# Hybrid decoder layer: gated results over the recurrence's and the convolution's tiles, squares in a buffer of their own

## The chip, the cores and the metric

One core of one Trainium2 chip runs the whole layer as one program. The metric is the device time of one execution in microseconds (us). The core has a matrix engine (TensorE, PE in the profile; its weight loads are PEld), a vector engine (VectorE, DVE), an engine for functions of one operand (ScalarE, ACT), a general engine (GpSimd, POOL), and SyncE (SP), which here issues nearly all transfers (DMA) between the chip's large memory (DRAM) and the on-chip tiles. Each engine executes its own instructions strictly in the order of the program; engines wait for each other by semaphores.

## What is computed

```python
D_MODEL, BATCH, SEQ = 1024, 1, 2048     # D_CONV = D_LRU = 1024
xn = rms_norm(x, ln_g)
proj = einsum('bsd,de->bse', xn, w_in)                  # 1024 -> 6144 columns
b_gate, c_gate, x_conv, g_conv, x_lru, g_lru = split(proj)
y_conv = b_gate * causal_depthwise_conv(c_gate * x_conv, conv_w)             # width 3
y_conv = headwise_rms_norm(y_conv, 8, conv_out_g) * silu(g_conv)
u = causal_depthwise_conv(x_lru, lru_conv_w) + lru_conv_b                    # width 4
r, i = sigmoid(heads(u) @ w_a + b_a), sigmoid(heads(u) @ w_i + b_i)
a = exp(8 * r * log_sigmoid(lam))
h_t = a_t * h_(t-1) + sqrt(1 - a_t^2) * (i_t * u_t)                          # scan over positions
y_lru = headwise_rms_norm(h, 16, lru_out_g) * silu(g_lru)
out = rms_norm(x + concat(y_conv, y_lru) @ w_out, final_g)
```

All of it is float32. The change concerns the two `headwise_rms_norm(...) * silu(...)`: the mean of squares of a head, and the product of a mixer's result with its gain and its gate. The factor 1/rms of a head is applied later, when the products are read back for the output projection.

## The kernel before

**Tiles and steps.** The channels lie on the 128 partitions, positions along a tile. The positions go in two halves of 1024, `h` = 0 and 1. A half of one block of 128 channels is a 128x1024 float32 tile. Float32 products are built from three matmuls of split operands (a high part `th` or `s`, a low part `tl`), and blocks of matrices are combined so that seven products do the work of eight (a step). There are 64 steps: in each half and for each of the eight channel blocks `k` a triple of three steps, `l` (columns of the recurrence and its gate), `a` and `b` (the convolution's columns and its gate); after the two halves 16 steps `o` of the output projection. A step has seven slots, one for each product (the eighth pass of a step's loop, where there is one, falls together with the next step's first); a triple has 21 slots. The first half splits its weights on the way, the second half reads the split inputs back from DRAM (`s<-sd`).

**What sets the order.** It is written by hand. `tick()` (L151) is called at each slot and issues what was put off by `at(n, f)`, n slots ago. The results of a product are combined by ACT copies (`q`, `u`, `rr`, L1234 to L1240) and DVE additions (`gl`, `gb`, `xl`, ... `<-bank`, L163) and so free the PSUM banks that TensorE writes next. Everything that is late on these two engines therefore reaches TensorE by way of `bank`.

**The tiles around the change.** In a triple, `lru` (L638) makes the recurrence: gates on TensorE (L680), Tanh, Exp and Sqrt on ACT, then on DVE the scan into tile `r` (one buffer, L714). `conv_a` and `conv_b` make the convolution's result in tile `t` (one buffer). The gates go to tiles `gl` (recurrence) and `gb` (convolution), which share two buffers and take turns; `silu` (L608) makes `g * sigmoid(g)` of them, with ACT for the sigmoid `sg` (L613, behind a table load) and POOL for the product.

`finish` (L593) ends a mixer's block: for the recurrence it is called at slot 17 after its last input and so acts from slot 2 of the next triple (`d0` = 0); for the convolution it is called with `d0` = 6 and acts from slot 7 of the next triple. It issues, in order of slots: `f1` (L595, DVE), the product of result, gain and gate, written over the gate tile; `store` (L600, SP), which writes that product to `yd` in DRAM in two transfers; the Square (L605, ACT), written over the result `y`; and `head_sums` (L586, DVE), a sum over channels of a head with a transposing reduction, whose input is read with a stride of 32 elements (128 bytes). When all 16 sums of a half are there, `head_norms` makes 1/rms with a few matmuls (`norm_ps`) and stores it to `rsd`.

**The ring "hl".** Four buffers of 128x1024 are handed out in turn under the tag `hl`: for the inputs at the start (`xrow`, `xcol`), the two `st` tiles of each recurrence, and the `so` tiles of `jobs`. `jobs()` (L363) prepares, during the second half from step 30 on, inputs of the output projection: it reads `yd` and `rsd` back, multiplies, combines, and for seven tiles in each of six jobs casts to a `so` tile (L421, ACT), subtracts (DVE) and stores it two slots later (L426, SP). `hl_tile` counts the tiles in use and `may()` (L352) holds a job's next tile back while the count is at 4 (at 2 in places 20 and 0 to 2 of a triple, and always in places 8 to 12):

```python
    def hl_tile(name, n=1):
        hlc[0] += n
        return [wt("hl", name, dt=F32R, bufs=HL) for _ in range(n)]

    def may():
        p = place[0]
        if 8 <= p <= 12:
            return False
        return hlc[0] < (2 if p >= 20 or p <= 2 else 4)
```

At the turn from the first half to the second, and from the second to the output projection, ACT also casts the next stage's weights (`th<-traw`, L280 and L458) and DVE makes their low parts (`tl`).

Of the kernel before, what the change touches and what calls it, by code (L numbers as in the profile page):

```python
# [12 lines left out]
F32 = mybir.dt.float32  # L13
F32R = mybir.dt.float32r
AF = mybir.ActivationFunctionType
# [5 lines left out]
C = 512  # L21
NC = S // C
NB = C // P
KT = D // P
EPS = 1e-6
PE = mybir.EngineType.PE
R = 32
# [11 lines left out]
def hymba_kernel(ctx: ExitStack, tc: tile.TileContext, x, xt, w_in, par, lamc, w_gate, w_out, final_g, out):  # L39
    nc = tc.nc  # L40
# [21 lines left out]
    def wt(tag, name, n=2 * C, dt=F32, bufs=1):  # L62
        return work.tile([P, n], dt, tag=tag, bufs=bufs, name=name)

    IG, O2, HL = 2, 2, 4
# [30 lines left out]
    for w in range(2):  # L96
        nc.gpsimd.tensor_tensor(out=sel[0][:, w * R:(w + 1) * R], in0=quarter[2 * w],
                                in1=quarter[2 * w + 1], op=ALU.add)
    nc.gpsimd.tensor_tensor(out=sel[1][:, 2 * R:], in0=sel[0].bitcast(F32)[:, 0:R],
                            in1=sel[0].bitcast(F32)[:, R:2 * R], op=ALU.add)  # L100
# [8 lines left out]
    hl = const.tile([P, KT], F32, name="hl")  # L109
# [34 lines left out]
    def at(slots, *fs):  # L144
        if slots == 0:
            for f in fs:
                f()
        else:
            due.append([slots, fs])
# [188 lines left out]

    hlc = [0]

    def hl_tile(name, n=1):
        hlc[0] += n
        return [wt("hl", name, dt=F32R, bufs=HL) for _ in range(n)]

    def hl_done(n):
        hlc[0] -= n
# [16 lines left out]
    def jobs():  # L363
        tjobs = [(t, j) for t in (2, 3) for j in range(NB)]
        for ph, m in ((0, 0), (0, 1), (1, 0), (1, 1), (0, 2), (0, 3)):
# [42 lines left out]
            for n, (i, v, after) in enumerate(items):  # L408
                if prev:
                    prev()  # L410
                    prev = None
                if n in (1, 5):
                    sums()
                if n in (2, 6):
                    more()
                if n == 4:
                    blocks()
                while not may():
                    yield
                t, = hl_tile("so")  # L420
                nc.scalar.copy(t[:, 0:C], v)  # L421

                def prev(t=t, i=i, v=v, after=after, dst=so[ph, m]):
                    tt(t[:, C:2 * C], v, t[:, 0:C].bitcast(F32), ALU.subtract)
                    after()
                    at(2, lambda: nc.sync.dma_start(  # L426
                        dst[i], t.bitcast(F32).rearrange("p (h c) -> p h c", h=2)))
                    at(3, lambda: hl_done(1))

                yield  # L430
# [111 lines left out]
    sums, summed = [None], [0]  # L542

    def head_norms(h):
        sm_ = sums[0]
        rt, = hl_tile("rt")
        rh, rl = rt[:, 0:C], rt[:, C:2 * C]
        at(4, lambda: hl_done(1))
        v = {}

        def split():
            nc.scalar.copy(rh, sm_)
            tt(rl, sm_, rh.bitcast(F32), ALU.subtract)

        def add():
            v["ps"] = pss.tile([P, C], F32, tag="s", name="norm_ps")[:NR, 0:KT * R]
            parts = [(n, q) for n in range(2) for q in (rh, rl)]
            for m, (n, q) in enumerate(parts):
                nc.tensor.matmul(v["ps"], sel[n], q[:, (1 - n) * KT * R:(2 - n) * KT * R],
                                 start=m == 0, stop=m == 3)  # L560

        def root():
            v["rs"] = aux("hn")[:NR, 0:KT * R]
            nc.scalar.activation(out=v["rs"], in_=v["ps"], func=AF.Sqrt, scale=inv_hd, bias=eps[:NR])

        def store():
            for w in range(3):
                k0 = (w + 1) % 3 * KT
                for i in range(2):
                    for b in range(NB):  # L570
                        p0 = w * R + (i * NB + b) * 4
                        nc.sync.dma_start(
                            rsd[h][i, b, k0:k0 + KT, :].rearrange("k (q r) -> q k r", q=4),
                            v["rs"][p0:p0 + 4].rearrange("q (k r) -> q k r", k=KT))
            normed[h] = True

        split()
        at(2, add)
        at(3, root)
        at(4, lambda: nc.vector.reciprocal(out=v["rs"], in_=v["rs"]))  # L580
        at(5, store)

    def head_sums(h, kt, y):
        if summed[0] == 0:
            sums[0] = psn.tile([P, 2 * KT * R], F32, tag="sums", name="sums")
        nc.vector.tensor_reduce(out=sums[0][:, kt * R:(kt + 1) * R], in_=y.rearrange("p (a r) -> p r a", r=R),  # L586
                                axis=mybir.AxisListType.X, op=ALU.add, apply_transpose=True)
        summed[0] += 1
        if summed[0] == 2 * KT:
            summed[0] = 0  # L590
            at(1, lambda: head_norms(h))

    def finish(d0, h, kt, y, sil, gain):  # L593
        def f1():
            nc.vector.scalar_tensor_tensor(out=sil, in0=y, scalar=gain, in1=sil,  # L595
                                           op0=ALU.mult, op1=ALU.mult)

        def store():
            for i in range(2):
                nc.sync.dma_start(yd[2 * h + i][:, :, kt, :].rearrange("b p t -> p b t"),  # L600
                                  sil[:, i * C:(i + 1) * C].rearrange("p (b t) -> p b t", b=NB))

        at(d0, f1)
        at(d0 + (1 if kt == KT and h == 0 else 2), store)
        at(d0 + 2, lambda: nc.scalar.activation(out=y, in_=y, func=AF.Square))  # L605
        at(d0 + 3, lambda: head_sums(h, kt, y))

    def silu(g, late=0):  # L608
        sg = [None]
# [28 lines left out]
    def lru(h, k, late=0):  # L638
# [22 lines left out]
        def sth():  # L661
            v["st"] = st = hl_tile("st", 2)
            at(6, lambda: hl_done(2))
            for j, hi in enumerate((LO, HI)):
                nc.scalar.copy(st[j][hi], v["u"][hi])
# [53 lines left out]
        def out_():  # L719
            finish(0, h, KT + k, v["r"], g, pt[:, LG + k:LG + k + 1])  # L720
# [65 lines left out]
    def conv_b(h, k):  # L786
        g = wt("o2", "gb", bufs=O2)

        def put(which, bank, other):
            t = tcur["t"]  # L790
            if which == 11 and other is None:
                tt(t[:, 0:C], bank, t[:, 0:C], ALU.mult)
            elif which == 11:
                tt(other, bank, other, ALU.add)
                tt(t[:, 0:C], other, t[:, 0:C], ALU.mult)
            elif which == 12 and other is None:
                tt(t[:, C:N2], bank, t[:, C:N2], ALU.mult)
            elif which == 12:
                tt(other, bank, other, ALU.add)
                tt(t[:, C:N2], other, t[:, C:N2], ALU.mult)  # L800
            else:
                combine(g[:, 0:C] if which == 21 else g[:, C:N2], bank, other)
            if which == 21:
                silu(g)
                finish(6, h, k, t, g, pt[:, CG + k:CG + k + 1])

        return put
# [126 lines left out]
    with tc.manual_schedule(engines={ENG.PE, ENG.Activation, ENG.DVE, ENG.Pool, ENG.SP}):  # L934
# [176 lines left out]
        for n in range(PLAIN, N):  # L1111
            kind, h, k = steps[n]
# [52 lines left out]
            for s in range(8 if new or last else 7):  # L1165
                i = ((0, 6) + ORDER[1:])[s]
# [59 lines left out]
                b = {0: "A", 1: "A", 2: "A", 5: "A", 3: "B", 6: "B", 4: "C"}[i]  # L1226
# [71 lines left out]
```

## Time and profile before

| | us |
|---|---|
| time before, median of 3 runs | 1403.29 (1401.82 to 1404.75) |
| the profiled execution | 1404.29 |
| its span in the trace | 1402.2 |

| engine | busy, us | share of the span |
|---|---|---|
| TensorE matmul | 1309.4 | 93% |
| VectorE | 1071.1 | 76% |
| ScalarE | 749.3 | 53% |
| GpSimd | 225.9 | 16% |

The granted TensorE clock was 0.981 of full speed on average. In the rows that follow, a group has line, engine, operation, tiles and shapes, then count, busy time, mean ns of one and the idle time ahead of it with its releasers. A row of the timeline has start, duration, engine, line, operation, tiles, and in brackets the idle time ahead of it and what ended it.

### The profile page before, as it was taken

The numbers are of one execution on the slowest core, as the hardware profiler recorded it, in microseconds if no ns is written. First come the engines' busy times: TensorE is split into PE (matmuls) and PEld (weight loads), VectorE is DVE, ScalarE is ACT, GpSimd is POOL, SyncE is SP. The second block draws the span as 40 slices with busy tenths as digits, with TensorE's granted clock in tenths as the row PEclk, the third lists the DMA queues.
The fourth block names the chain that finished last, engine by engine and source line by source line (L and its number), as shares of the span: only waits on it lengthen the run. The fifth ranks groups of instructions, "written<-read, shape, count | busy, mean of one in ns | idle before, by whom it ended". The sixth has DMA issues, their size and how long they took to land.

```text
span 1402.2 us, 16765 instructions
## 1 busy us (share of the span) xinstructions
PE 1309.4 (93%) x5612; PEld 1056.3 (75%) x5612; DVE 1071.1 (76%) x1274; ACT 749.3 (53%) x1135; POOL 225.9 (16%) x160
## 2 busy tenths in 40 slices
PE   6989999999999997899998998999998989989997
PEld 5867777787877775678876876787886868867886
DVE  6778888798989889778677787666649447658885
ACT  7475767566565756375563545354556123344443
POOL 2204233233433330101010110101010000000000
PEclk9999999999999998999999999999999999999999
DMA  5147698888988875631899999989878798698643
GB/s 216 30 142 252 255 284 238 288 321 274 337 289 311 307 259 205 230 112 43 292 374 356 389 350 385 343 275 323 286 278 275 286 297 256 220 403 296 216 153 138
DMA packets 166485, 371.00 MB, mean 265 GB/s; under 512 B 18944, under 2 KB 53760, under 8 KB 166400
## 3 DMA queue, kind: packets, MB, share of 16 engines
q1 hardware_dynamic: 166112, 369.63, 76.1%
q8 instruction: 44, 0.72, 0.2%
q14 instruction: 41, 0.34, 0.1%
q10 hardware_dynamic: 288, 0.32, 0.1%
HBM read 224.45 MB, written 145.43 MB: 264 GB/s over the span
## 4 chain that ended last, share of the span: by engine, by line
PE 43%; DMA 19%; DVE 14%; ACT 6%; issue 6%; SPq 2%; POOL 1%; DVEq 0%; ACTq 0%; POOLq 0%
PE bank L900 42%; DMA s<-so 3%; DMA zr<-rsd 3%; DVE s L163 3%; DMA sd<-s 3%; DMA yd<-gl 2%; DVE sums L586 2%; PE gate L680 2%; ACT i L687 2%; ACT r L687 1%; DMA traw<-td 1%; DMA so<-so 1%; DVE u L654 1%; DMA raw<-in_w_in_dram 1%; DMA s<-sd 1%
## 5 line engine op out<-in xcount | busy, mean ns | idle before, releaser
L900 PE MATMUL bank<-th,s 128*128 128x512 f32 x3608 | 1142.2, 395 | 47.8 <-ACT q L1234 12.6
L900 PEld LDWEIGHTS bank<-th,s 128*128 128x128 f32 x3608 | 685.8, 190 | 207.9 <-ACT q L1234 15.6
L900 PE MATMUL bank<-tl,s 128*128 128x512 f32 x1804 | 710.7, 394 | 10.2 <-DVE tl L163 9.9
L900 PEld LDWEIGHTS bank<-tl,s 128*128 128x128 f32 x1804 | 343.0, 190 | 86.4 <-DVE tl L163 15.2
L163 POOL TENSOR_TENSOR s<-raw,s 128x512 fp32r<-128x512 f32 x62 | 110.3, 1791 | 251.3 <-ACT s L200 221.1
L1237 ACT COPY u<-bank 128x512 f32<-128x512 f32 x58 | 34.0, 587 | 168.6 <-PE bank L900 69.6
L200 ACT CAST s<-raw 128x512 fp32r<-128x512 f32 x136 | 82.1, 616 | 64.1 <-PE bank L900 44.2
L163 DVE TENSOR_TENSOR tl<-traw,th 128x512 fp32r<-128x512 f32 x102 | 69.8, 712 | 41.8 <-ACT th L458 24.9
L163 POOL TENSOR_TENSOR gb<-gb,sg 128x1024 f32<-128x1024 f32 x16 | 40.8, 2553 | 351.1 <-ACT sg L613 292.8
L163 DVE TENSOR_TENSOR s<-s,s 128x512 fp32r<-128x512 f32 x102 | 88.9, 871 | 7.9 <-ACT s L200 7.9
L163 DVE TENSOR_TENSOR s<-raw,s 128x512 fp32r<-128x512 f32 (+1 forms) x120 | 85.0, 731 | 10.0 <-ACT s L200 5.3
L1234 ACT COPY q<-bank 128x512 f32<-128x512 f32 x58 | 33.9, 584 | 87.1 <-PE bank L900 70.3
L200 ACT CAST s<-s 128x512 fp32r<-128x512 f32 x102 | 62.8, 616 | 14.6 <-DVE s L163 10.6
L163 DVE TENSOR_TENSOR raw<-raw,zr 128x512 f32<-128x512 f32 x64 | 44.5, 721 | 29.7 <-DMA zr<-rsd 29.6
L654 DVE SCALAR_TENSOR_TENSOR u<-xl,pt,u 128x1024 f32<-128x1024 f32 x48 | 62.3, 1297 | 2.0 <-ACT u L650 1.5
L1240 ACT COPY rr<-bank 128x512 f32<-128x512 f32 x58 | 33.8, 583 | 49.1 <-PE bank L900 49.0
L764 DVE SCALAR_TENSOR_TENSOR t<-p,pt,t 128x1024 f32<-128x1024 f32 x32 | 47.6, 1488 | 8.5 <-ACT t L761 7.7
L163 DVE TENSOR_TENSOR ob<-bank,rr 128x512 f32<-128x512 f32 x18 | 12.2, 689 | 45.2 <-ACT rr L1240 45.2
L163 DVE TENSOR_TENSOR st<-u,st 64x1024 fp32r<-64x1024 f32 x32 | 45.5, 1422 | 1.0
L687 ACT ACTIVATE r<-gate,pt 64x512 f32<-64x512 f32 x64 | 43.8, 684 | 2.3 <-PE gate L680 1.6
L680 PE MATMUL gate<-st,bh 128*128 128x512 f32 x64 | 28.9, 452 | 16.7 <-DVE st L163 6.8
L687 ACT ACTIVATE i<-gate,pt 64x512 f32<-64x512 f32 x64 | 43.8, 684 | 1.1
(159 smaller groups left out, 1279.2 us busy)
## 6 DMA issues: line engine op xcount, KB each, us to landing
sd<-s SPq DMA_DIRECT2D x147, 512.0 KB
s<-sd SPq DMA_DIRECT2D x147, 512.0 KB
raw<-in_w_in_dram SPq DMA_DIRECT2D x108, 256.0 KB
so<-so SPq DMA_DIRECT2D x42, 512.0 KB
s<-so SPq DMA_DIRECT2D x42, 512.0 KB
raw<-yd SPq DMA_DIRECT2D x64, 256.0 KB
traw<-in_w_out_dram SPq DMA_DIRECT2D x56, 256.0 KB
yd<-gl SPq DMA_DIRECT2D x32, 256.0 KB
```

What stands on the lines that cost most here:

```text
L163: (eng or nc.vector).tensor_tensor(out=out, in0=a, in1=b, op=op)
L200: nc.scalar.copy(dst[i][0], val(i))
L586: nc.vector.tensor_reduce(out=sums[0][:, kt * R:(kt + 1) * R], in_=y.rearrange("p (a r) -> p r a", r=R), axis=mybir.AxisListType.X, op=ALU ...
L654: nc.vector.scalar_tensor_tensor(out=v["u"], in0=o1[:, 1 + j:1 + j + N2], scalar=lw[j], in1=v["u"], op0=ALU.mult, op1=ALU.add)
L680: nc.tensor.matmul(ps[j], v["gw"][n][:, j, :], v["st"][j][:, sl], start=(n == 0), stop=(n == 1))
L687: nc.scalar.activation(out=g_[hi, sl], in_=v["ps"][j][src], func=AF.Sigmoid, bias=pt[src, bias + k:bias + k + 1])
L764: nc.vector.scalar_tensor_tensor(out=tcur["t"], in0=p[:, 2 + j:2 + j + N2], scalar=cw[j], in1=tcur["t"], op0=ALU.mult, op1=ALU.add)
L900: nc.tensor.matmul(bank, a[:, js], b, start=start and n == 0, stop=stop and n == 2, skip_group_check=more)
L1234: nc.scalar.copy(q1, bk["A"])
L1237: nc.scalar.copy(u2, bk["A"])
L1240: nc.scalar.copy(rr, bk["A"])
```

## The change

`hl_tile` takes a type. `finish` allots a tile `sq` from the ring `hl` and squares `y` into it at `d0`; the Square writes it in another order of elements (stride 32), so that `head_sums`, now at `d0 + 2`, reads each sum's 32 elements in a row. `f1` stands at `d0 + 1` and writes the gated product over `y`, that is over `r` or `t`. The store reads `y` and stands at `d0 + 3` in all cases, and the `sq` tile is counted as done at `d0 + 3`.

```diff
@@ -338,9 +338,9 @@
-    def hl_tile(name, n=1):
+    def hl_tile(name, n=1, dt=F32R):
         hlc[0] += n
-        return [wt("hl", name, dt=F32R, bufs=HL) for _ in range(n)]
+        return [wt("hl", name, dt=dt, bufs=HL) for _ in range(n)]
@@ -583,7 +583,7 @@
-        nc.vector.tensor_reduce(out=sums[0][:, kt * R:(kt + 1) * R], in_=y.rearrange("p (a r) -> p r a", r=R),
+        nc.vector.tensor_reduce(out=sums[0][:, kt * R:(kt + 1) * R], in_=y.rearrange("p (r a) -> p r a", a=R),
                                 axis=mybir.AxisListType.X, op=ALU.add, apply_transpose=True)
@@ -591,19 +591,26 @@
     def finish(d0, h, kt, y, sil, gain):
+        def square():
+            sq[0], = hl_tile("sq", dt=F32)
+            nc.scalar.activation(out=sq[0].rearrange("p (r a) -> p a r", a=R),
+                                 in_=y.rearrange("p (a r) -> p a r", r=R), func=AF.Square)
+
         def f1():
-            nc.vector.scalar_tensor_tensor(out=sil, in0=y, scalar=gain, in1=sil,
+            nc.vector.scalar_tensor_tensor(out=y, in0=y, scalar=gain, in1=sil,
                                            op0=ALU.mult, op1=ALU.mult)
 
         def store():
             for i in range(2):
                 nc.sync.dma_start(yd[2 * h + i][:, :, kt, :].rearrange("b p t -> p b t"),
-                                  sil[:, i * C:(i + 1) * C].rearrange("p (b t) -> p b t", b=NB))
-
-        at(d0, f1)
-        at(d0 + (1 if kt == KT and h == 0 else 2), store)
-        at(d0 + 2, lambda: nc.scalar.activation(out=y, in_=y, func=AF.Square))
-        at(d0 + 3, lambda: head_sums(h, kt, y))
+                                  y[:, i * C:(i + 1) * C].rearrange("p (b t) -> p b t", b=NB))
+
+        sq = [None]
+        at(d0, square)
+        at(d0 + 1, f1)
+        at(d0 + 2, lambda: head_sums(h, kt, sq[0]))
+        at(d0 + 3, store)
+        at(d0 + 3, lambda: hl_done(1))
```

No engine gets more or fewer instructions. Three places show how the order moves.

DVE around the first block's end (first half, second triple), before. `gl<-bank,rr` fills the next gate tile; `s` are split inputs:

```order
L595 SCALAR_TENSOR_TENSOR gl<-r,pt,gl 128x1024
L163 TENSOR_TENSOR s<-s_1047,s 128x512
L163 TENSOR_TENSOR gl<-bank,rr 128x512
L595 SCALAR_TENSOR_TENSOR gb<-t,pt,gb 128x1024
L163 TENSOR_TENSOR s<-raw,s 128x512
L163 TENSOR_TENSOR s_1047<-raw,s_1047 128x512
L163 TENSOR_TENSOR xl<-bank,q_1036 128x512
L586 TENSOR_REDUCE sums<-r 128x32
L163 TENSOR_TENSOR s<-s_1045,s 128x512
L586 TENSOR_REDUCE sums<-t 128x32
```

The same place after:

```order
L600 SCALAR_TENSOR_TENSOR r<-r,pt,gl 128x1024
L163 TENSOR_TENSOR s<-s_1047,s 128x512
L163 TENSOR_TENSOR gl<-bank,rr 128x512
L586 TENSOR_REDUCE sums<-sq 128x32
L163 TENSOR_TENSOR s<-raw,s 128x512
L163 TENSOR_TENSOR s_1047<-raw,s_1047 128x512
L163 TENSOR_TENSOR xl<-bank,q_1036 128x512
L600 SCALAR_TENSOR_TENSOR t<-t,pt,gb 128x1024
L163 TENSOR_TENSOR s<-s_1045,s 128x512
L586 TENSOR_REDUCE sums<-sq 128x32
```

The recurrence's sum has moved ahead of the next inputs' splits, the convolution's product behind them.

ACT at the turn from the first half to the second, before. `th<-traw` are casts of the second half's weights, `sg<-gb` is the last sigmoid of the first half:

```order
L280 CAST th<-traw 128x512 x2
L644 COPY xl<-hx 128x4
L613 ACT_TABLE_LOAD
L613 ACTIVATE sg<-gb 128x1024
L280 CAST th<-t_4493 128x512
L280 CAST th<-traw 128x512 x7
L605 ACTIVATE r<-r 128x1024
L280 CAST th<-traw 128x512 x14
L1149 COPY q_4844<-bank 128x512
L605 ACTIVATE t<-t 128x1024
```

The same place after:

```order
L280 CAST th<-traw 128x512 x2
L651 COPY xl<-hx 128x4
L596 ACTIVATE sq<-r 128x32x32
L620 ACT_TABLE_LOAD
L620 ACTIVATE sg<-gb 128x1024
L280 CAST th<-t_4507 128x512
L280 CAST th<-traw 128x512 x14
L596 ACTIVATE sq<-t 128x32x32
L280 CAST th<-traw 128x512 x7
L1156 COPY q_4861<-bank 128x512
```

The recurrence's Square has moved from behind eight casts to ahead of the table load; the convolution's has moved ahead of seven casts.

ACT in one triple of the second half with jobs, before:

```order
L421 CAST so<-raw 128x512 x2
L1237 COPY u_7287<-bank 128x512
L613 ACT_TABLE_LOAD
L613 ACTIVATE sg<-gb 128x1024
L605 ACTIVATE r<-r 128x1024
L1240 COPY rr<-bank 128x512
L743 COPY xl<-bank 128x512
L650 ACTIVATE u<-xl,pt 128x1024
L1234 COPY q_7409<-bank 128x512
L605 ACTIVATE t<-t 128x1024
```

The same triple after:

```order
L596 ACTIVATE sq<-r 128x32x32
L1244 COPY u_7281<-bank 128x512
L620 ACT_TABLE_LOAD
L620 ACTIVATE sg<-gb 128x1024
L421 CAST so<-raw 128x512 x2
L1247 COPY rr<-bank 128x512
L421 CAST so<-raw 128x512 x2
L750 COPY xl<-bank 128x512
L596 ACTIVATE sq<-t 128x32x32
L657 ACTIVATE u<-xl,pt 128x1024
```

The two Squares stand ahead of the copy of `u` and of `u<-xl`, where they stood behind the sigmoid and behind the next step's `q`, and four `so` casts lie where none did. With the `sq` tiles in the ring the six jobs begin and end one or two slots apart from before, their order being the same.

## The prediction

> **What bounds the kernel now.** I read the page first, then busy times by stretch, then the waits, then the groups of one stretch.
>
> ```profile
> PE 1309.4 (93%) x5612; PEld 1056.3 (75%) x5612; DVE 1071.1 (76%) x1274; ACT 749.3 (53%) x1135; POOL 225.9 (16%) x160
> core 0: us, PE busy (x) PEld busy (x) DVE busy (x) ACT busy (x) POOL busy (x), PEclk, DMA share, GB/s
> 690.00:1030.00 340.00, 322.72 (x1378) 260.29 (x1377) 238.84 (x265) 165.38 (x224) 34.93 (x23) 0.98 0.95 338
> 260.00:500.00 240.00, 236.05 (x1028) 191.82 (x1027) 218.11 (x223) 151.42 (x221) 92.04 (x58) 1.00 0.88 309
> ```
>
> TensorE (PE) is the bound. A steady stretch of the first half (260 to 500 us) needs 240.00/1028 = 0.233 us per matmul; the stretch of the second half in which the jobs run (690 to 1030) needs 340.00/1378 = 0.247. At the first pace the second would take 1378 x 0.233 = 322 us, so about **18 us** are lost there. In the first half VectorE (DVE) is busy 218.11/240 = 91%: delays there eat its slack.
>
> ```profile
> DVE gl L163 <- DMA yd<-gl: 35.5, 8, 8.0
> ACT so L421 <- DMA so<-so: 23.6, 5, 8.4
> L900 PE MATMUL bank<-th,s 128*128 128x512 f32 x892 | 282.4, 395 | 12.3 <-ACT q L1234 7.3 <-DMA s<-sd 2.8 <-ACT u L1237 1.9
> L680 PE MATMUL gate<-st,bh 128*128 128x512 f32 x20 | 9.2, 459 | 4.9 <-DVE st L163 3.8 <-ACT i L687 1.1
> ```
>
> The first two rows are waits over the whole span (us in total, times, longest): DVE stands 35.5 us until the store of a gated result has read its "gl" tile, and ScalarE (ACT) 23.6 us until a "so" store has read its tile of the four-deep "hl" ring. The next two are TensorE's groups in 690 to 1030, with the idle time before them: 7.3 behind ACT's q, 1.9 behind u and 3.8 behind DVE's st come from late DVE and ACT work, 13.0 together; 2.8 is a plain load.
>
> **Part 1: the wait on the store of gl.** The result now lies in r, so gl is free once f1 has read it, and no store stands ahead of DVE's next write. What one such wait costs shows in the first triple:
>
> ```profile
> 116.49 0.69 DVE L163 TENSOR_TENSOR gl<-bank,rr 128x512 f32<-128x512 f32 x1 [2.85 <-DMA yd<-gl]
> 129.41 0.68 DVE L163 TENSOR_TENSOR gl<-bank,u 128x512 f32<-128x512 f32 x1
> 130.19 0.59 ACT L1237 COPY u<-bank 128x512 f32<-128x512 f32 x1 [6.52 <-DVE gl L163]
> 130.82 0.80 PE L900 MATMUL bank<-th,s 128*128 128x512 f32 x1 [2.48 <-ACT u L1237]
> 131.42 0.63 PE L900 MATMUL bank<-tl,s 128*128 128x512 f32 x1
> 131.84 0.63 PE L900 MATMUL bank<-th,s 128*128 128x512 f32 x1
> ```
>
> DVE loses 2.85 at 116.49, is full from there on (no idle time ahead of 129.41), and so u is copied late and TensorE stands 2.48. After it matmuls start 131.84 - 131.42 = 0.42 apart instead of 0.23; I estimate seven to eight such starts from the length of the stall, 1.4 us. With the wait gone, 129.41 comes by 126.6, and stall and slow starts go: at most 3.9. I take **-3.5**.
>
> What takes the store's place is a wait of r's next writer on the store of r, and t's on the store of t. By the order, nine and six slots of 2.8 us (12 x 0.233) lie between, 25 and 17 us; issue to landing took under 7 us in the row of part 4. Those two stay covered, at nothing; if a store took 17 us, the conv's writes of t would stand. The later yd stores pass a few SP issues only and are read a whole half later: nothing.
>
> **Part 2: squares and sums.**
>
> ```profile
> L586 DVE TRANSPOSE_TENSOR_REDUCE sums<-t 128x32 f32<-128x1024 f32 x16 | 33.8, 2110 | 0.0
> L586 DVE TRANSPOSE_TENSOR_REDUCE sums<-r 128x32 f32<-128x1024 f32 x16 | 33.4, 2090 | 0.0
> L595 DVE SCALAR_TENSOR_TENSOR gl<-r,pt,gl 128x1024 f32<-128x1024 f32 x16 | 24.1, 1506 | 0.1
> L595 DVE SCALAR_TENSOR_TENSOR gb<-t,pt,gb 128x1024 f32<-128x1024 f32 x16 | 20.3, 1270 | 0.0
> L605 ACT ACTIVATE t<-t 128x1024 f32<-128x1024 f32 x16 | 17.0, 1061 | 4.7 <-DVE gb L595 4.6
> L605 ACT ACTIVATE r<-r 128x1024 f32<-128x1024 f32 x16 | 16.8, 1053 | 3.5 <-DVE gl L595 3.4
> ```
>
> The counts stay: 32 gatings, 32 Squares, 32 sums. The sums read 1024 elements 128 bytes apart in 2.10 us; afterwards they read in a row, which no row shows for this operation. Bounds: 2.10 (no change) and 1.27 (the contiguous 128x1024 operation). Square costs 1.06 and now writes 128 bytes apart: 1.06 to 1.06 x 2.10/1.27 = 1.75. I take 1.27 and 1.75, the strided reader being the nearest row: DVE gains 32 x 0.83 = 27 us, ACT gives 32 x 0.69 = 22. ACT is busy 151.42 of 240, and TensorE waits there for neither queue for long (pace 0.233), so this is **0** in steady triples; where DVE is late it is a small gain, counted in part 4. [...]
>
> **Part 3: the two turns between stages.** Square now waits for the scan, at the gating's old place, ahead of the table load, sg and the weight casts in ACT's order.
>
> ```profile
> 539.52 2.28 DVE L714 TENSOR_TENSOR_SCAN r<-r,u 128x1024 f32<-128x1024 f32 x1
> 541.91 3.12 DVE L595 SCALAR_TENSOR_TENSOR gl<-r,pt,gl 128x1024 f32<-128x1024 f32 x1
> 544.96 0.68 DVE L163 TENSOR_TENSOR tl<-t,th 128x512 fp32r<-128x512 f32 x1
> 535.98 1.28 ACT L613 ACT_TABLE_LOAD   x1
> 539.64 1.06 ACT L613 ACTIVATE sg<-gb 128x1024 f32<-128x1024 f32 x1 [2.38 <-DVE gb L163]
> 540.61 0.60 ACT L280 CAST th<-t 128x512 fp32r<-128x512 f32 x1
> 540.78 3.17 POOL L163 TENSOR_TENSOR gb<-gb,sg 128x1024 f32<-128x1024 f32 x1 [15.34 <-ACT sg L613]
> 546.29 0.80 PE L900 MATMUL bank<-tl,s 128*128 128x512 f32 x1 [4.01 <-DVE tl L163]
> ```
>
> Before, sg and the cast of th were done while the scan ran, and TensorE stood 4.01 for DVE's tl, behind the scan and a gating of 3.12 (1.27 elsewhere; it overlaps GpSimd's (POOL) gb*sg). After: scan to 541.8, Square to 542.9-543.5, table load (1.28) and sg to 545.2-545.9, th done 545.8-546.4. POOL's 3.17 then starts near 545.3 and lies beside tl instead of the gating. Taking what the gating lost (1.85) as lost by tl, tl moves from 544.96 to about 547.6: **+2.6**; without that collision +0.9. [...]
>
> ```profile
> 1066.53 1.12 ACT L458 CAST th<-traw 128x512 fp32r<-128x512 f32 x2
> 1067.91 3.12 DVE L595 SCALAR_TENSOR_TENSOR gl<-r,pt,gl 128x1024 f32<-128x1024 f32 x1
> ```
>
> The second turn has the same order; a DMA wait behind it takes up part: **+2**, bounds 0 and 2.6. Together +4.6.
>
> **Part 4: the stretch 690 to 1030.**
>
> ```profile
> 885.75 1.18 SPq L600 DMA_DIRECT2D yd<-gl  x2
> 887.02 0.62 SPq L426 DMA_DIRECT2D so<-so  x1
> 891.99 0.69 DVE L163 TENSOR_TENSOR gl<-bank,rr 128x512 f32<-128x512 f32 x1 [7.95 <-DMA yd<-gl]
> 892.16 0.59 ACT L743 COPY xl<-bank 128x512 f32<-128x512 f32 x1 [4.80 <-PE bank L900]
> 895.35 1.25 ACT L650 ACTIVATE u<-xl,pt 128x1024 f32<-128x1024 f32 x1 [2.60 <-DVE xl L163]
> 896.50 0.56 ACT L1234 COPY q<-bank 128x512 f32<-128x512 f32 x1
> ```
>
> Six of the eight gl waits lie here; they go. What TensorE lost to late ACT and DVE is 13.0 plus slow starts behind the large stalls, within the 18 of the first part. The other cause of these 13 stays (ACT's wait for "so" stores, below), so I take half of the 18: **-9**, bounds 0 and -18. Against more speaks the DMA share 0.95.
>
> Square adds two tiles per triple to the hl ring. In five triples the square of t reuses the tile of the "so" cast four slots earlier, whose store issues like the 887.02 row. A landing as slow as yd's (885.75 to 891.99, 6.2 us) gives 893.3 to 894.5; Square's place is behind xl, 892.75. ACT would stand 0.5 to 2 us and has idle 2.60 and the q copy until 896.50. Covered, at nothing; without the cover it costs what the slower rival says.
>
> **Sum:** -3.5 + 0 + 4.6 - 9 = -7.9. The profiled execution took 1404.29 us, its span being 1402.2; the median of the three times is 1403.29, 1.0 less. From 1403.29: 1395.
>
> **The rivals.**
>
> *DMA holds the job stretch.* The stretch moves 338 GB/s at a share of 0.95, and loads set the pace once DVE no longer does. Part 4 is then 0, the sum +1.1: 1404. For it: the 0.95, and 2.8 of TensorE's idle time already behind s<-sd. Against it: the slices of the page reach 403 GB/s.
>
> *Slower: the hl ring.* Stores of "so" land later than 894.5 in that picture, and ACT's queue stands at Square with xl, u and q behind it. The price is in the trace, where ACT stood for such a store:
>
> ```profile
> 760.24 0.62 ACT L421 CAST so<-raw 128x512 fp32r<-128x512 f32 x1 [7.77 <-DMA so<-so]
> 766.40 0.80 PE L900 MATMUL bank<-th,s 128*128 128x512 f32 x1 [4.83 <-ACT q L1234]
> ```
>
> 7.77 for one "so" cast, and TensorE 4.83 later on, with slow starts and the second late operation about 8 us (estimate). Five squares at 8 are +40, less part 4's full 18 and with parts 1 and 3 (+1.1): 1426; at half that price 1406. It decides where a store lands more than some 3 us behind Square's place (892.75 + 3, while q is due by 897.7). Against it: the landing of 6.2. For it: 23.6 us of such waits exist already, in the same ring.
>
> *Contiguous sums shift more than the wait.* If 27 us of DVE time count where DVE is late (st, tl), part 4 reaches -18 and the turns cost +0.9 each: -3.5 + 1.8 - 18: 1384. Against: TensorE waits for DVE in few places.
>
> *The wait isn't removed:* gl's writer then waits for f1 instead, a slot later. f1 took 1.27 to 1.5 and stands on the same engine in order, so this can't stall DVE; I give it no chance of its own.
>
> **How the numbers follow.** Forecast (1387 to 1400, all faster): 0.45. DMA-bound, 1401 to 1407: 0.2. Ring, 1406 to 1430: 0.22. Contiguous sums, 1378 to 1387: 0.13. 0.2% is 2.8 us, about what a measurement of this kernel can tell from no change. Faster (under 1400.5): 0.45 + 0.13 and nothing of the DMA case: 0.58. Within (1400.5 to 1406.1): 0.18 of the DMA case and 0.01 of the ring: 0.19. Slower: 0.02 + 0.21 = 0.23. The range leaves out the lower part of the third rival (0.07) and the upper part of the ring (above 1414, 0.12): 1381 to 1414. The likeliest case alone: 1387 to 1400.
>
> **What would show it.** Right: no row of gl waiting on a yd store; the stall at 130.82 gone; TensorE's idle time behind q and u in the job stretch well under 9; tl at the first turn some 2 us later against the scan's start; sums at 1.3 or less, Square above 1.06. Wrong: Square in the list of waits behind "so" stores with more than 10 us (ring); the stretch as long as before with its idle time behind s<-sd or raw (DMA); sums still at 2.1; r or t waiting on a yd store.

## The result

The change makes the kernel slower: 1414.51 us (median of 4 runs, 1411.14 to 1416.77) against 1403.45 (4 runs), a ratio of 1.0074 with a 95% interval of 1.0053 to 1.0096. The profiled execution has a span of 1413.0, 10.8 more than before. The forecast was 1395 with a range of 1381 to 1414.

The page of the changed kernel, its stretch 690 to 1030 and its waits over the whole span (us in total, times, longest):

```profile
PE 1314.8 (93%) x5612; PEld 1062.0 (75%) x5612; DVE 1060.1 (75%) x1274; ACT 778.9 (55%) x1135; POOL 228.8 (16%) x160
690.00:1030.00 340.00, 320.14 (x1362) 259.94 (x1361) 229.35 (x262) 171.78 (x218) 31.39 (x22) 0.97 0.94 332
ACT sq L596 <- DVE r L721: 44.4, 15, 6.9
ACT sq L596 <- DMA so<-so: 20.8, 5, 7.3
DVE t L600 <- ACT sq L596: 20.4, 8, 3.8
```

The wait of gl on the yd store, 35.5 us before, is gone. Three others have come. Two are at the new Square: 44.4 us for the scan (r, L721) and 20.8 for so stores. The third is VectorE's (DVE): the gating writes over t, which Square reads, and so stands for Square, 20.4 us in all. In 340 us of the job stretch 1362 matmuls start, before 1378.

Where the time went is read most simply from the starts of the same matmul in two traces. Each row is the difference changed minus before that a stage adds (worked out from the starts of the first and the last matmul of the stage). It comes from one profiled execution of each kernel: stages whose own program an edit left alone have differed by 2 to 3 us between two profiles, so differences of that size are not told apart.

| stage (us in the trace of before) | forecast | measured |
|---|---|---|
| first triple's end, 115 to 139 | -3.5 | -4.4 |
| rest of the first half, 139 to 524 | 0 | -0.6 |
| first turn, 524 to 603 | +2.6 | +4.3 |
| job stretch, 662 to 1057 | -9 | +3.7 |
| second turn, 1057 to 1152 | +2 | +7.5 |
| all other | 0 | +0.2 |
| sum | -7.9 | +10.7 |

The squares and sums of the changed kernel, by shape:

```profile
L586 DVE TRANSPOSE_TENSOR_REDUCE sums<-sq 128x32 f32<-128x1024 f32 x32 | 40.0, 1249 | 0.0
L596 ACT ACTIVATE sq<-r 128x1024 f32<-128x1024 f32 x16 | 34.0, 2124 | 44.4 <-DVE r L721 44.4
L596 ACT ACTIVATE sq<-t 128x1024 f32<-128x1024 f32 x16 | 33.6, 2101 | 20.8 <-DMA so<-so 20.8
```

The sums fell from 2.10 to 1.25 us, the Square rose from 1.06 to 2.1. ScalarE (ACT) at the first turn, changed kernel:

```profile
530.41 0.19 ACT L651 COPY xl<-hx 128x4 f32<-128x4 f32 x1
536.48 1.93 ACT L596 ACTIVATE sq<-r 128x1024 f32<-128x1024 f32 x1 [5.88 <-DVE r L721]
538.42 1.28 ACT L620 ACT_TABLE_LOAD   x1
539.71 1.06 ACT L620 ACTIVATE sg<-gb 128x1024 f32<-128x1024 f32 x1
540.67 0.60 ACT L280 CAST th<-t 128x512 fp32r<-128x512 f32 x1
```

VectorE, GpSimd and TensorE there, and the first of the two TensorE rows in the kernel before:

```profile
541.31 2.44 DVE L163 TENSOR_TENSOR tl<-t,th 128x512 fp32r<-128x512 f32 x1 [4.67 <-ACT th L280]
540.85 2.36 POOL L163 TENSOR_TENSOR gb<-gb,sg 128x1024 f32<-128x1024 f32 x1 [21.28 <-ACT sg L620]
541.85 0.80 PE L907 MATMUL bank<-th,s 128*128 128x512 f32 x1 [6.57 <-ACT th L280]
544.41 0.80 PE L907 MATMUL bank<-tl,s 128*128 128x512 f32 x1 [1.76 <-DVE tl L163]
541.78 0.50 PE L900 MATMUL bank<-th,s 128*128 128x512 f32 x1 [1.14 <-ACT th L280]
```

ScalarE stands 5.88 us at Square with the table load, sg and the cast that TensorE waits for behind it. The cast starts at the same place on the clock as before (540.67 beside 540.61), though all before it ran 5.3 us ahead. TensorE waits 6.57 + 1.76 here where it waited 1.14 + 4.01.

### The profile page after: what moved, and what is told of

Read it like the earlier page. It is cut to its first block, busy times and chain, and to the rows that moved or that the text cites. A ratio compares the mean times of both kernels' runs of the same rounds, so it can differ in the third digit from the quotient of the medians.

```text
span 1413.0 us, 16779 instructions
## 1 busy us (share of the span) xinstructions
PE 1314.8 (93%) x5612; PEld 1062.0 (75%) x5612; DVE 1060.1 (75%) x1274; ACT 778.9 (55%) x1135; POOL 228.8 (16%) x160
## 5 line engine op out<-in xcount | busy, mean ns | idle before, releaser
L907 PEld LDWEIGHTS bank<-tl,s 128*128 128x128 f32 x1804 | 344.8, 191 | 84.8 <-DVE tl L163 12.9
L163 DVE TENSOR_TENSOR s<-raw,s 128x512 fp32r<-128x512 f32 (+1 forms) x120 | 85.6, 736 | 10.7 <-ACT s L200 3.7
L163 DVE TENSOR_TENSOR s<-s,s 128x512 fp32r<-128x512 f32 x102 | 84.8, 832 | 1.3 <-ACT s L200 1.3
L661 DVE SCALAR_TENSOR_TENSOR u<-xl,pt,u 128x1024 f32<-128x1024 f32 x48 | 65.7, 1368 | 0.8 <-ACT u L657 0.2
L596 ACT ACTIVATE sq<-r 128x1024 f32<-128x1024 f32 x16 | 34.0, 2124 | 44.4 <-DVE r L721 44.4
L163 DVE TENSOR_TENSOR traw<-traw 128x512 f32<-128x512 f32 x57 | 42.5, 745 | 18.4 <-DMA traw<-in_w_out_dram 17.5
L163 DVE TENSOR_TENSOR st<-u,st 64x1024 fp32r<-64x1024 f32 x32 | 51.0, 1595 | 1.0
L163 DVE TENSOR_TENSOR raw<-raw 128x512 f32<-128x512 f32 x52 | 47.5, 914 | 0.6
L163 POOL TENSOR_TENSOR gl<-gl,sg 128x1024 f32<-128x1024 f32 x16 | 41.2, 2576 | 29.8 <-ACT sg L620 29.8
```

What stands on the lines that cost most here:

```text
L163: (eng or nc.vector).tensor_tensor(out=out, in0=a, in1=b, op=op)
L596: nc.scalar.activation(out=sq[0].rearrange("p (r a) -> p a r", a=R), in_=y.rearrange("p (a r) -> p a r", r=R), func=AF.Square)
L661: nc.vector.scalar_tensor_tensor(out=v["u"], in0=o1[:, 1 + j:1 + j + N2], scalar=lw[j], in1=v["u"], op0=ALU.mult, op1=ALU.add)
L907: nc.tensor.matmul(bank, a[:, js], b, start=start and n == 0, stop=stop and n == 2, skip_group_check=more)
```

## The experiments

Ratios are to the kernel before, run beside it on the same chip, with 95% intervals. "Stage" differences are worked out as in the table above.

### The turns

*The last block of each half finishes as before* (in the changed kernel):

```diff
     def finish(d0, h, kt, y, sil, gain):
+        if kt % KT == KT - 1:
+            return finish_old(d0, h, kt, y, sil, gain)    # finish of the kernel before
```

> The changed kernel, but the last block of each half (k = 7, recurrence and convolution) finishes as before: gating first, into the gate tile, Square behind. Theory A (at both turns Square ahead of the weight casts holds ScalarE for the scan): turn one gives back 3 to 4 us and turn two 5 to 7, the rest stays: 1403 to 1407 us. Rival (the turns are late because stores and loads moved, not because of ScalarE's order): 1412 to 1416.

1404.04 us, 1.0003 (0.9987 to 1.0018): the whole loss is gone with 2 of 16 blocks. First turn +1.0 in place of +4.3, second -2.4 in place of +7.5; the job stretch keeps its +3.9.

*The change at the last block of each half alone* (in the kernel before, the condition turned round):

> The kernel before, with the change applied to the last block of each half alone. Theory A: 8 to 12 us more than before at the two turns, 1411 to 1415 us. Rival (the turns were late because the blocks ahead of them were changed too): 1402 to 1406.

1413.78 us, 1.0069 (1.0043 to 1.0095): the whole loss again. Turns +3.2 and +6.1, and at the first the same row of waits:

```profile
542.05 1.93 ACT L615 ACTIVATE sq<-r 128x1024 f32<-128x1024 f32 x1 [5.88 <-DVE r L740]
543.99 1.28 ACT L639 ACT_TABLE_LOAD   x1
545.28 1.06 ACT L639 ACTIVATE sg<-gb 128x1024 f32<-128x1024 f32 x1
546.24 0.60 ACT L280 CAST th<-t 128x512 fp32r<-128x512 f32 x1
```

*The end of the last block two slots later* (changed kernel; its data flow stays, ScalarE's order at the turns becomes the old one):

```diff
     def finish(d0, h, kt, y, sil, gain):
+        if kt % KT == KT - 1:
+            d0 += 2
```

> The changed kernel, with everything that the last block of each half does at its end (Square, gating, sum, store) put two slots later, so that ScalarE's order at the turns is the old one: sigmoid and weight casts first, Square behind. The data flow of the change stays (gating over r and t, squares in the ring). Theory A (ScalarE's order at the turns is the loss): as far back as undoing the last block was, 1402 to 1407 us. Rival (the gating over r or t, or the ring's tile at the turn, is the loss): 1411 to 1416.

1401.35 us, 0.9977 (0.9964 to 0.9991). Turns -1.7 and -0.4. TensorE at the first:

```profile
536.27 0.49 PE L910 MATMUL bank<-th,s 128*128 128x512 f32 x1 [1.13 <-ACT th L280]
539.65 0.61 PE L910 MATMUL bank<-tl,s 128*128 128x512 f32 x1 [2.88 <-DVE tl L163]
```

So the gating over r and t does not cost at the turns as such. The edit moves gating, sum and store along with Square; that Square's place in ScalarE's queue is what counts is read from the rows above, where TensorE waits for the cast and the cast stands behind Square. Two lines that put off the end of each half's last block make the change slightly faster than before.

*The layout undone* (changed kernel; Square in order, sums with the stride):

```diff
-in_=y.rearrange("p (r a) -> p r a", a=R)                     # head_sums
+in_=y.rearrange("p (a r) -> p r a", r=R)
-nc.scalar.activation(out=sq[0].rearrange("p (r a) -> p a r", a=R),
-                     in_=y.rearrange("p (a r) -> p a r", r=R), func=AF.Square)
+nc.scalar.activation(out=sq[0], in_=y, func=AF.Square)
```

> The changed kernel with the layout alone undone: Square writes its elements in order, the sums read with a 128-byte stride again. Theory A: Square falls from 2.1 to 1.06 us, the sums rise from 1.25 to 2.1, each turn gets about 1 us shorter, the job stretch stays within 3 us: 1410 to 1414 us. Rival B (a Square of twice the length is the main loss): 1403 to 1407. Rival C (the short sums are worth something to VectorE): slower than the changed kernel, 1416 to 1422.

1414.62 us, 1.0066 (1.004 to 1.0091), not told apart from the changed kernel. Turns +2.6 and +6.2, about 1.5 less each, too little for the medians to show. The layout is neither the loss nor a gain that the times show.

### The ring

*Ring tiles alone* (in the kernel before, a 128x1 operation on a tile of the ring at the slots of Square):

```diff
+        def ring():
+            t, = hl_tile("sq")
+            nc.scalar.activation(out=t[:, 0:1], in_=gain, func=AF.Square)
+        at(d0, ring)
+        at(d0 + 3, lambda: hl_done(1))
```

> The kernel before, with two more tiles per triple taken from the four-deep ring hl at the slots where the change takes them, each written by a 128x1 operation on ScalarE (nothing else of the change). Theory A (the ring: an so store must land before the tile is reused, and that costs the job stretch): ScalarE waits on so stores in 690 to 1030 for more than the 23.6 us of before, that stretch is 3 to 10 us longer, first triple and both turns as before: 1406 to 1414 us. Rival B (the ring is harmless, the changed kernel's stretch is lost to the later and longer Square): within 2 us of before, 1401 to 1406.

1402.65 us, 0.9986 (0.9968 to 1.0005): no loss that can be measured; the stretch +1.4. Its ScalarE waits on so stores add up to 20.2 at the new operation and 9.2 at the casts, 29.4 against 23.6: mostly moved, not added, and the yd waits fell from 32.2 to 11.3 beside it. The time is as rival B had it, and my theory was too simple: more waiting on so stores alone did not make the stretch 3 to 10 us longer.

*Squares in the recurrence's tile u* (changed kernel; u is free between the scan and the next block's start, if the convolution's Square comes two slots earlier):

```diff
-            sq[0], = hl_tile("sq", dt=F32)
+            sq[0] = wt("u", "sq")
...
-        at(d0, square)
+        dq = d0 - (2 if d0 and h + kt else 0)
+        at(dq, square)
         at(d0 + 1, f1)
-        at(d0 + 2, lambda: head_sums(h, kt, sq[0]))
+        at(dq + 1, lambda: head_sums(h, kt, sq[0]))
         at(d0 + 3, store)
-        at(d0 + 3, lambda: hl_done(1))
```

> The changed kernel with the squares in the recurrence's free tile u in place of the ring; for that the convolution's Square and sum stand two and three slots earlier; the ring and its count are as before. Theory A: ScalarE no longer waits for an so store at Square, the job stretch falls below the one of before (the waits on the yd store are gone too): 4 to 14 us less than the changed kernel, 1400 to 1410, turns still long. Rival (DMA sets the pace of the stretch): it keeps its length within 2 us, 1412 to 1416.

1411.45 us, 1.0055 (1.0033 to 1.0076), with an interval that overlaps the changed kernel's. It lies between the ranges of theory and rival. The stretch +1.2 in place of +3.7, not below the one of before, with no yd wait left; the first turn is longer (+6.6), the second shorter (+4.7) than in the changed kernel. This pair does not show a price of the ring: 2.5 us between two profiles is no more than they differ by without a cause. The next kernel does.

*Squares in u and the last blocks as before*: what remains is the yd waits taken away.

> Squares in u and the last block of each half as before: what is left of the change is the waits on the yd store taken away in the other blocks. Theory A (both losses are taken away and the job stretch is held by so stores, not by the yd waits): first triple 4 us shorter, stretch as before within 2, 1398 to 1402 us. Rival B (my prediction's part 4, the yd waits cost TensorE 9 us there): 1388 to 1396.

1397.06 us, 0.9943 (0.9919 to 0.9968), between the ranges of theory A and rival B. The stretch is only 1.7 us shorter than before (its program is that of the kernel above, with +1.2 there, so two profiles differ by some 3 us). By the starts the rest of the gain lies in the first half (-3.9 at the first triple, -4.7 after it) and in the second turn (-4.0); but the profiled execution was the shortest of six, 6.8 us under their median, so these add up to 13.7 us where the medians are 7.0 apart.

But for the tile of the squares and the convolution's Square two slots earlier, this is the kernel of *The last block of each half finishes as before*: 0.9943 beside 1.0003, with intervals that lie apart. So the squares in the ring did cost some 7 us (1404.04 less 1397.06); in the stretch the two profiles have -1.7 beside +3.9. How much of it is ScalarE's wait for so stores and how much VectorE's gating standing for a late Square (13.7 us at t in the stretch with the ring, none with u) was not taken apart.

With the layout undone as well:

> Squares in u and the last block of each half as before, and the layout undone too: Square in order (1.06 us), sums with the 128-byte stride (2.1 us). Theory A (neither engine's length matters away from the turns): within 3 us of the same kernel with the changed layout, 1394 to 1400 us. Rival (ScalarE's 2.1 us per Square still costs in the job stretch and in the first half): 1386 to 1393. Rival (the sums' length on VectorE costs): 1401 to 1406.

1395.28 us, 0.9941 (0.9919 to 0.9963), the same within the interval.

### What holds the job stretch

*The yd store one slot earlier* (kernel before, `at(d0 + 1, store)` in all blocks):

> The kernel before with the store of every gated result one slot earlier, nothing else. VectorE's waits on the yd store in 690 to 1030 fall from 32 us towards 15. Theory A (those waits lie in VectorE's slack there): the stretch keeps its length within 2 us, 1401 to 1405 us. Rival B (my part 4): half of the 9 us, 1397 to 1400. Rival C (SyncE waits for the gating on VectorE and holds up loads): 1406 to 1412.

The yd waits in the stretch fell from 32.2 to 6.8 us and it got 2.2 us shorter. The time is 1408.13 (1.0041; 1.0017 to 1.0065) all the same; SyncE stands 105.0 us over the span for the gating on VectorE at this store (68.8 and 36.2), where it stood 40.0 (27.4 and 12.6). The profiled execution was among its shortest (+1.0 by the starts, with +3.6 in the first half after the first triple), so where the others lose it is not shown.

*The so store one slot earlier* (kernel before, `at(1, ...)` in place of `at(2, ...)` at L426), and the same in the kernel with squares in u and old last blocks:

> The kernel before with the so store of the jobs issued one slot earlier, nothing else. Theory A (what TensorE loses in the job stretch hangs on so stores landing late in front of ScalarE's queue): the 23.6 us of so waits fall by 10 or more, the yd waits stay above 20, the stretch gets 4 to 8 us shorter: 1395 to 1399 us. Rival B (the yd waits hold it): stretch within 2 us, 1401 to 1405. Rival C (SyncE now waits for VectorE's subtraction and holds up loads): slower, 1405 to 1415.

> Squares in u, the last block of each half as before, and the so store one slot earlier. Theory A (SyncE waits for VectorE's subtraction as it did in the kernel before with that one edit, whatever VectorE's waits on the yd store): 3 to 7 us more than without the early store, 1400 to 1405 us. Rival (VectorE, rid of the yd waits, is early enough): 2 to 6 us less, 1391 to 1395.

Both lose: 1408.88 us, 1.0037 (1.002 to 1.0055), and 1402.8, 0.9998 (0.9978 to 1.0017) where 0.9943 stood without it. The so waits did fall, from 23.6 to 5.6 in the first, but SyncE's queue stood instead, for VectorE's subtraction (first kernel, SyncE's waits over the span; 10.5 us before):

```profile
SPq L426 <- DVE so L163: 66.8, 30, 5.2
```

*Each so tile counted as in use two slots longer* (in the kernel with squares in u, old last blocks and old layout): the job then holds its next cast back, where ScalarE's whole queue stood at that cast for a store.

```diff
-                    at(3, lambda: hl_done(1))     # in jobs
+                    at(5, lambda: hl_done(1))
```

> The kernel with squares in u, the old end of each half's last block and the old layout, and in addition each so tile counted as in use for two slots more, so that a job holds its next cast back until the store has landed, where ScalarE's whole queue stood for it. Theory A (what TensorE still loses in the job stretch hangs on ScalarE standing for so stores): the so waits fall from 21.5 us below 5, the stretch gets 3 to 7 us shorter, 1388 to 1393 us. Rival (the jobs end later and the output projection waits for their tiles, or the loss only moves to another late engine): 1394 to 1400.

**1374.07 us, 0.9785 (0.9756 to 0.9814)**, the fastest of all. Its job stretch, the waits on so stores that ScalarE has left in it, and TensorE's main group with the idle time ahead of it:

```profile
690.00:1030.00 340.00, 337.29 (x1475) 275.85 (x1473) 249.63 (x277) 181.96 (x248) 34.54 (x23) 1.00 0.98 351
ACT so L421 <- DMA so<-so: 3.6, 3, 1.6
L924 PE MATMUL bank<-th,s 128*128 128x512 f32 x951 | 296.2, 390 | 1.4 <-ACT q L1258 0.8 <-ACT rr L1264 0.3
```

1475 matmuls in 340 us, 0.231 each, the pace of the first half; the stage is 22.7 us shorter than before and 21 shorter than in the kernel without the hold, three times the 3 to 7 that I had expected. TensorE's idle time in the 340 us, with the 1.3 ahead of the gates' matmuls, is 2.7 us where it was 17.2 (12.3 and 4.9), and the granted clock is 1.00 where it was 0.98, which is worth some 7 of 340 us (an estimate from these two clocks): together most of the 22.7. DMA moved 351 GB/s here, so 338 was no ceiling. The hold also spaces out the jobs' loads and stores; that this helped beside ScalarE's queue is not ruled out.

*The same hold alone in the kernel before*, where the yd waits stay, and *the hold in the changed kernel with late last blocks*, where the squares stay in the ring:

> The kernel before with the hold alone: each so tile counted as in use for two slots more. The waits on the yd store stay. Theory A (the whole loss of the stretch was ScalarE standing for so stores, the yd waits lie in VectorE's slack): the stretch gets 18 to 23 us shorter here as well, 1380 to 1386 us. Rival (the yd waits bind as soon as the so waits are gone): at most half of it, 1390 to 1398.

> The changed kernel with the end of each half's last block two slots later and the hold; the squares stay in the ring. If the ring costs only by so stores that have not landed, Square waits for them less than 5 us in all and the time comes near the best one, 1374 to 1382 us. If the two squares still meet so stores in the ring: 1385 to 1398.

1383.45 us, 0.9853 (0.983 to 0.9876), the stage 18.2 shorter; and 1382.36, 0.985 (0.9829 to 0.9871), 13.7 shorter. The stretch of the first and its waits:

```profile
690.00:1030.00 340.00, 335.56 (x1457) 273.48 (x1456) 252.98 (x275) 173.93 (x237) 38.38 (x23) 0.99 0.96 346
DVE gl L163 <- DMA yd<-gl: 12.9, 6, 4.9
ACT so L421 <- DMA so<-so: 4.8, 2, 2.6
```

Holding the casts back also cut the yd waits from 32.2 to 12.9: part of them had followed from the so waits. In the second kernel ScalarE's squares still met so stores, which puts it between my two cases (ScalarE's wait in the stretch; TensorE stood 5.7 us behind q there):

```profile
ACT sq L599 <- DMA so<-so: 8.5, 3, 6.8
```

## Why the prediction was wrong

**Part 1, first triple: right.** Forecast -3.5, measured -4.4, somewhat above its "at most 3.9". The row that was to come by 126.6 did:

```profile
113.30 0.68 DVE L163 TENSOR_TENSOR gl<-bank,rr 128x512 f32<-128x512 f32 x1
126.06 0.68 DVE L163 TENSOR_TENSOR gl<-bank,u 128x512 f32<-128x512 f32 x1
```

No wait of r or t on a yd store appeared.

**Part 2: right in its sum, wrong in one bound.** The sums measured 1.25 (taken: 1.27). Square measured 2.1, above its upper bound of 1.75: the bound scaled a VectorE ratio. Undoing the layout moved the time by nothing measurable, so this was not the error.

**Part 3, the turns: mechanism and place right, size wrong by more than half.** Forecast +4.6, measured +11.8. ScalarE's order was read rightly: by the working the cast was to start 4.6 to 5.2 us late (545.2 to 545.8 in place of 540.61) and started 5.4 late (540.67, with 5.3 us of lead lost). At the first turn the sum went on from the shorter of its two Squares (th done at 545.8), though part 2 takes the longer one; from 546.4 the same sum gives +3.3, and the tl matmul came 3.4 late (544.41, in place of 546.29 less the lead). Slow starts behind it (0.42 to 0.43 us apart until 552.94, in the kernel before until 553.54) make it 4.1 at the tl matmul of 553.55 (554.73 before); the stage ends at +4.3.

The step that failed is the size of the second turn, "+2, bounds 0 and 2.6", with "a DMA wait behind it takes up part". TensorE's idle time there, three rows of the changed kernel and two of the kernel before (1085.89 is the same matmul as 1096.60):

```profile
1077.27 0.51 PE L907 MATMUL bank<-th,s 128*128 128x512 f32 x1 [1.75 <-ACT th L458]
1082.25 0.79 PE L907 MATMUL bank<-tl,s 128*128 128x512 f32 x1 [4.48 <-DVE tl L163]
1096.60 0.77 PE L907 MATMUL bank<-th,s 128*128 128x512 f32 x1 [3.99 <-DMA s<-so]
1080.68 0.50 PE L900 MATMUL bank<-tl,s 128*128 128x512 f32 x1 [2.85 <-DVE tl L163]
1085.89 0.47 PE L900 MATMUL bank<-th,s 128*128 128x512 f32 x1 [1.05 <-DMA s<-so]
```

The waits on th and tl grew from 3.5 to 6.4 us in all, and the wait on s<-so did not shrink: it grew from 1.05 to 3.99. SyncE stood longer for tl ahead of its next weight loads (over the span, changed kernel; 17.5, 17, 5.5 before):

```profile
SPq L450 <- DVE tl L163: 30.7, 21, 9.9
```

The s<-so load that it issued at 1081.44 before came at 1088.82, 4.0 us later by the matmuls, which ran 3.4 us late here even ahead of the turn. So the rows point to late casts that reach TensorE a second time, by SyncE's ordered queue; this path was not tried by itself. Also not counted were the slow starts after these longer stalls (0.42 us apart in place of 0.23; the granted clock over 1057 to 1152 was 0.90, before 0.96), as in part 1. The lengthening of tl beside GpSimd that the first turn's +2.6 counts on (1.85 us, what the gating lost there) came nearly in full: tl took 2.44 us beside GpSimd's 2.36 and 0.68 elsewhere, 1.76 more.

**Part 4, the job stretch: the step that failed is "I take half of the 18: -9".** VectorE's 32 us of waits on the yd store stood mostly in its slack. Taken away with the so waits left, they were worth 1.7 us (squares in u, old last blocks) and 2.2 (early yd store) by the profiles, no more than profiles differ by. TensorE's 3.8 us behind st, which the prediction put to late engines, did not hang on them either: with squares in u and no yd wait left it still stood 4.4 to 5.8 us there. In the changed kernel the sign that was named, "idle time behind q and u in the job stretch well under 9", went the other way: 15.4 and 2.6, 18.0 together.

```profile
PE bank L907 <- ACT q L1241: 15.4, 3, 5.6
```

The other cause, ScalarE's queue standing at a buffer whose so store has not landed, was nearly the whole loss: the hold alone, in the kernel before with its yd stores as they were, made the stage 18.2 us shorter (the yd waits that fell with it included), and 18 were lost by the pace of the first half. What the yd waits cost once that is gone is at most the 4.5 between 22.7 and 18.2, in which the squares' place in u has its share too.

The second step that failed in part 4 is "Covered, at nothing": Square did stand for so stores in five triples, 20.8 us in all.

```profile
762.24 1.93 ACT L596 ACTIVATE sq<-t 128x1024 f32<-128x1024 f32 x1 [7.31 <-DMA so<-so]
765.71 0.79 PE L907 MATMUL bank<-th,s 128*128 128x512 f32 x1 [5.62 <-ACT q L1241]
829.42 1.96 ACT L596 ACTIVATE sq<-t 128x1024 f32<-128x1024 f32 x1 [5.25 <-DMA so<-so]
832.91 0.61 PE L907 MATMUL bank<-th,s 128*128 128x512 f32 x1 [4.56 <-ACT q L1241]
```

This is the slower rival, with its place and mechanism, at a lower price than its 8 us for each of five squares: some 7 us in all by the times of the kernels with and without the ring. So casts waited 23.6 us before and only 5.2 now, so that most of the wait was moved, and three of the five waits (7.31, 5.25 and 6.59; the other two are under 1) reached TensorE. VectorE's gating standing for Square, which the prediction doesn't list, is part of this price or beside it.

**The rivals.** DMA as the bound at 338 GB/s is out: 351 were moved when ScalarE no longer stood. Contiguous sums as a gain are out. The sign was missed by adding a wrong -9 to a turn that was sized at less than half. The time lies in the ring rival's range (1406 to 1430) by luck: by the stages the turns added 11.8 us, where that sum has them at 4.6, and the job stretch only 3.7.

## What to carry to other kernels

Before crediting the end of a wait, ask which engine's waits TensorE's own idle time hangs on in that stretch: 32 us of VectorE's waits were worth about 2, 24 us of ScalarE's were worth 18 with the VectorE waits that fell along with them. An instruction that waits in an engine's ordered queue holds up what stands behind it (5.88 us at Square at the first turn, with the cast behind it that TensorE waited 6.57 us for), so an operation moved ahead of others should be placed by when its input is ready, above all at the turns between stages, where the next stage's weights stand in the same queue. A ring's "in use" count should last until the store has landed; then the producer yields and its engine hardly stands (3.6 and 4.8 us of 23.6 were left).

## What the runs showed of the hardware

A Square of 128x1024 float32 on ScalarE took about 2.1 us on average when it wrote with a 128-byte stride and 1.06 in order, twice as long; the transposing sum on VectorE took about 2.1 with such a stride in its input and 1.25 without. Behind TensorE's stall of 2.48 us in the first triple of the kernel before (until 130.82) the granted clock over 130.4 to 133.6 us was 0.50, and over 764 to 773, with the stall of 4.83 in it, it was 0.62: these stalls cost more than their length. Shorter waits can cost: both stores that were issued one slot earlier made the kernel slower by 0.4%, with SyncE's ordered queue standing for VectorE (66.8 us at the so store, 105.0 at the yd store) in place of the wait that was removed.
